# Reciprocal root by a power on GpSimd, and columns spread by transposition, in a two-block mixer network

## The chip, the cores and the metric

The kernel runs on one core of a Trainium2 chip. The core has five engines with queues of their own: TensorE (PE in the profile; its weight loads are PEld), VectorE (DVE), ScalarE (ACT), GpSimd (POOL) and SyncE (SP), which issues most DMAs. The metric is the device time of one execution in microseconds; lower is better.

## What is computed

The input is x of 512 tokens with 1024 features and a context of 256 tokens. A first block mixes tokens by retention and by an mLSTM, both in two directions, and ends in a gated feed-forward part; a second block has four layers: latent attention, windowed attention, long convolutions, latent attention. What matters here are the norms, which stand at many places (before and after each layer, per head behind the retention and the mLSTM, on the compressed queries and keys of the latent attention):

```python
def rms_norm(x, gain):
    xf = x.astype(jnp.float32)
    y = xf * lax.rsqrt(jnp.mean(xf * xf, axis=-1, keepdims=True) + EPS)
    return (y * gain.astype(jnp.float32)).astype(x.dtype)

def head_norm(t):
    tf = t.astype(jnp.float32)
    return tf * lax.rsqrt(jnp.mean(tf * tf, axis=-1, keepdims=True) + EPS)
```

Also of matter are the places where a number per token divides a whole row: the sums of the softmax in both attentions, and the denominator of the mLSTM, h = num / max(|den|, exp(-m)).

## The kernel before

Activations lie with the features on the partitions and the tokens along the free axis, in tiles of [128, 512] for x and [128, 256] for the context. Every fp32 operand of the large products is kept as two halves (a rounded one and the rest), so a product is three matmuls (`mac`, L438 to L440). Weights come by DMA from SyncE's queue and are split into halves by ScalarE (L394) and VectorE (L395).

A norm goes in three steps. `Rms.add` squares a tile on ScalarE (L231) and sums on VectorE (L235). `Rms.root` turns the sums into a column per 128 tokens: on TensorE the sum over the partitions, with the tile of sums as stationary operand and a column of ones as moving one (L242); on ScalarE the root with its scale and eps (L244); on VectorE the reciprocal (L245). `Rms.rstd` then calls `over_columns`, which spreads columns over the partitions: column j, repeated 128 times by its access pattern, is the stationary operand, the identity is the moving one, and the fp32 product has the column along the free axis of every partition (L1370). VectorE multiplies with it (L567 in `apply`, L1305 behind a mixer's output product, L899 for the heads).

There are 44 roots, 13 of four columns and 31 of two, so 114 columns named rs. `over_columns` has three other callers: the latent attention (L1602) spreads the reciprocal sums of the softmax (rd) with four columns per head for x and, in the first of its layers, two per head for the context; the windowed attention (L1741) spreads four per unit, of which there are 24 (6 for each of 4 groups); the mLSTM (L1015) spreads its denominators (den), four columns for each of 4 heads and 2 directions. That makes 176 columns of rd and 32 of den.

The order of work is written with generators: `weave` lets several streams take turns at given shares, so that the steps of a norm stand between the products of another stream. Constants such as D5, D6, E0 and E2 set how many steps lie between a root and its use. At the end of a layer (`layer_end`), the product of one group of 256 tokens is woven with the norm of the group before. The framework that builds the program then sets the order on each engine's queue from the order of the code and an estimate of its own, and puts in the waits and ScalarE's table loads.

Of the kernel before, what the change touches and what calls it, by code (L numbers as in the profile page):

```python
# [18 lines left out]
D = 1024  # L19
# [158 lines left out]
def mix(*items):  # L178
    """Takes turns between generators: (generator, its number of steps), each at its share."""
    live = [[g, n, 0] for g, n in items if g is not None and n]  # L180
    while live:
        x = min(live, key=lambda x: x[2] / x[1])
        try:
            next(x[0])
        except StopIteration:
            live.remove(x)
            continue
        x[2] += 1
        yield
# [7 lines left out]
def idle(n):  # L197
    """Steps without work."""
    for _ in range(n):
        yield  # L200
# [21 lines left out]
class Rms:  # L222
    """Sums of squares over the partitions of some tiles [128, n]."""

    def __init__(self, k, n, width, eps=None):
        self.k, self.n, self.width, self.acc, self.cols = k, n, width, None, None
        self.eps = k.eps if eps is None else eps
# [9 lines left out]
    def root(self):  # L237
        """Columns of 1/rms: tokens on the partitions."""
        nc, nt = self.k.nc, self.n // 128
        ps = self.k.mm()  # L240
        for j in range(nt):
            nc.tensor.matmul(ps[:, j:j + 1], self.acc[:, 128 * j:128 * j + 128], self.k.ones1, start=True, stop=True)  # L242
        s = self.k.sp.tile([128, 8], F32, tag="rs", name="rs")
        nc.scalar.activation(s[:, :nt], ps[:, :nt], AF.Sqrt, bias=self.eps, scale=1.0 / self.width)  # L244
        nc.vector.reciprocal(s[:, 4:4 + nt], s[:, :nt])  # L245
        self.cols = [s[:, 4 + j:5 + j] for j in range(nt)]

    def rstd(self):
        """PSUM [128, n] of 1/rms on every partition."""
        if self.cols is None:  # L250
            self.root()
        return self.k.over_columns(self.cols, 128)


class Kern:
# [15 lines left out]
    def setup(self):  # L271
# [28 lines left out]
        self.eps = self.cp.tile([128, 1], F32, name="eps")  # L300
        nc.vector.memset(self.eps, EPS)
        self.eps4 = self.cp.tile([128, 1], F32, name="eps4")
        nc.vector.memset(self.eps4, 4 * EPS)
# [15 lines left out]
    def rows(self, late, dma):  # L319
        """Columns of the small vectors, of the first group or the others."""  # L320
# [23 lines left out]
        if not late:  # L344
            # silu of the conditioning vectors as padded stationary columns
# [34 lines left out]
    def acts(self, kt, n):  # L380
        """kt feature tiles [128, n] in two halves."""
# [15 lines left out]
    def wload(self, W, r0, kt, c0, n):  # L397
        """Rows r0.. (kt tiles) and columns c0.. of W, f32 [128, kt, n]."""
# [9 lines left out]
    def wm(self, W, r0, kt, c0, n=128):  # L408
        """kt tiles [128, n] of W in two exact halves."""
# [4 lines left out]
    def wheld(self, W, c0, slot, r0=0, kt=KT):  # L414
        """wm of 128 columns, held in two to four tiles of another pool if one is given."""
# [13 lines left out]
    def wv(self, W, c0):  # L429
        """The same for 256 columns of all D rows."""  # L430
        return self.wm(W, 0, 4, c0, 256) + self.wm(W, 512, 4, c0, 256)

    def mac(self, ps, pairs, start=True, stop=True):
        """ps (+)= sum over pairs (l, r) of l^T r with both halves of each."""
# [7 lines left out]
    def proj(self, w, act, n, c0=0, m=128):  # L442
        """PSUM [m, n] = (columns c0.. of w)^T act, act [kt] of [128, n]."""
# [4 lines left out]
    def proj_t(self, act, t0, w, ps):  # L448
        """ps [128 tokens, cols] = act[:, t0..]^T w."""
        self.mac(ps, [(a[:, t0:t0 + 128], x) for x, a in zip(w, act)])  # L450

    def lead(self, loads, h, late, first=None):
        """PSUM [128, N] of three products (of weights, 128 columns) with h; `late` makes its second half of tokens, `first` runs before."""
# [19 lines left out]
    def load_T(self, src, n, dst):  # L473
        """Feature tiles dst[k] [128, n] of src [n, D]."""
# [17 lines left out]
    def mod(self, W, w0, cond, bias, dst_x, dst_c):  # L492
        """Columns w0..w0+1023 of W (f32, [1024, .]) applied to both conditioning vectors, plus bias columns."""
# [23 lines left out]
    def mod_stream(self):  # L517
        """All modulation vectors in their order of use, in steps."""
# [21 lines left out]
    def mods(self, n):  # L540
        """The next n steps of the stream, as an item to weave."""
# [7 lines left out]
    def rstd(self, xs, n, width):  # L549
        """PSUM [128, n] of 1/rms over the partitions and tiles of xs."""  # L550
# [5 lines left out]
    def rstd1(self, x, f):  # L556
        """Head norm sums of one tile, to be finished later: 1 / sqrt(f * mean + 4 * eps)."""
        r = Rms(self, N, DH / f, self.eps4)
# [3 lines left out]
    def apply(self, x, bc, n, G, S, dst, kt):  # L562
        """dst halves = x * G * bc + S, per feature tile; S None: no shift."""
# [35 lines left out]
    # ================= first block =================  # L599
    def first_block(self):  # L600
# [68 lines left out]
        def gates():  # L669
# [27 lines left out]
            # rows, forward on [0:4] and backward on [32:36]: input gates, log forget gates  # L697
            # (context: halves of one tile)
# [37 lines left out]
            # rows to spread over the partitions: B - m on [0:64], exp(B + m0 - m) on [64:128]  # L736
# [5 lines left out]
            # columns: exp(-m)  # L742
# [7 lines left out]
            # columns: exp(i - B + ...) of the context, i - B of x  # L750
# [32 lines left out]
        def kv_ctx(w):  # L783
            """Token-major keys or values of the context for a pair of heads, f32 [128, 2, 256]."""
# [10 lines left out]
        def dense(pair, ml):  # L795
            """Projections of two heads: K, V, the context's states, q, gate."""
# [80 lines left out]
        def scores(K, q):  # L877
            """S^T of all blocks: four PSUM banks [128 keys, N]."""
# [16 lines left out]
        def finish():  # L895
            """The head norm of the head before."""
# [4 lines left out]
        def ret_chain(pair):  # L901
            o = out[pair, False]
            for u in range(2):
                h = 2 * pair + u
                # decays between tokens on two overlapping strips, columns 0..511 and 384..895
# [46 lines left out]
        def ml_chain(pair):  # L952
            o = out[pair, True]
            for u in range(2):
# [46 lines left out]
                for d in range(2):  # L1001
                    # 1 / max(|den|, exp(-m)) with the tokens on the partitions: the rows of den are all the same
# [80 lines left out]
        def passes(W, r0, kt, act, gate, slots, rs, ws):  # L1083
            """X += gate * act^T W for the first half of the tokens, then for the other."""
# [83 lines left out]
        def norm3(g):  # L1168
            """The first block's last norm, and the next layer's."""
# [22 lines left out]
    # ================= second block =================  # L1192
# [20 lines left out]
    def keep(self, i, k, x, t0):  # L1213
        """Halves of the tokens t0.. of tile k (6 or 7) of a mixer's output, for its product."""
# [8 lines left out]
    def preload(self, l, W):  # L1223
        """The first weights of a mixer's output product."""
# [7 lines left out]
    def load_acts(self, i, t0, a):  # L1232
        """Halves of 256 tokens of the mixer's output tiles that are in DRAM, two tiles in one."""
# [7 lines left out]
    def layer_end(self, l, W, tail):  # L1241
        """Output product of a layer's mixer, the residuals, and the norm of the next layer, in groups of 256 tokens: the last one's pending.
        The mixer's last steps are woven with the first product."""
# [86 lines left out]
    def store(self, ys, t0, c0):  # L1330
        """256 tokens of four feature tiles to the output."""
# [16 lines left out]
    def rope64(self, ps):  # L1348
        """ps [128 = two heads of 64, N] with the axial rotation, f32."""
# [8 lines left out]
    def stacks(self, r, n, d0, d1):  # L1358
        """Halves of two heads of 64 rows over each other: d0 = [hi; lo] of r[0:64], d1 = [lo; hi] of r[64:128]."""
# [6 lines left out]
    def over_columns(self, cols, m):  # L1366
        """PSUM [m, 128 * len]: each column [128, 1] along the free axis of every partition."""
        ps = self.mm()
        for i, c in enumerate(cols):
            self.nc.tensor.matmul(ps[:m, 128 * i:128 * i + 128], c.to_broadcast([128, m]), self.ident, start=True, stop=True)  # L1370
        return ps[:m, :128 * len(cols)]

    def softmax(self, S, P, rd, scale, sink=None):
        """P = exp(scale * S - its maximum), rd = 1 / its sums over the free axis (with a further column `sink`)."""
# [13 lines left out]
    def transposed(self, blocks):  # L1388
        """[128, 128 * len] halves of the transposes of f32 blocks [128, 128]."""
# [8 lines left out]
    def stream_tiles(self, items, lag):  # L1398
        """Dense tiles: items of (weights, use for x, use for the context or None), the context's `lag` tiles behind;
# [703 lines left out]
```

## Time and profile before

| what | us |
|---|---|
| median of 3 runs | 2951.34 (2949.51 to 2959.04) |
| span of the profiled execution | 2954.9 |
| TensorE busy in it | 2825.0 (96%) |
| VectorE busy | 1819.6 (62%) |
| ScalarE busy | 1395.2 (47%) |
| GpSimd busy | 85.8 (3%) |

The rows further down come from one profiled execution. In its views, a row of a timeline gives the start of a group of instructions, their length, engine, line, operation, what is written and read, the count, and in brackets how long the engine had been idle and what ended that. Matmuls overlap, so what one costs is read from the distance between starts, not from its length. An engine's busy share is an average over stretches with different limits, so the table of stretches is read beside it.

### The profile page before, as it was taken

Reading aid. Unit: us, or ns where it says so; the run is one execution under the profiler, and the core shown is the slowest. Engines: PE = TensorE matmul, PEld = TensorE weight load, DVE = VectorE, ACT = ScalarE, POOL = GpSimd, SP = SyncE. Lnnn points to the kernel's source line nnn. Section 1 sums busy time; section 2 is a strip of 40 time slices with the busy share of each in tenths; the row PEclk is TensorE's granted clock in tenths of the full one; section 3 lists DMA queues with packets and bytes.
Section 4 is the critical chain, followed back from the end, with each engine's and each line's share of the span. In section 5 each row is a group of like instructions: output and inputs, shape, how many; then the busy total and the mean of one; then the engine's idle time right before and its main releaser. Section 6 shows DMA issues by size and latency. Waiting matters only on the chain. (4 is left out here: it accounts for less than half of the span.)

```text
span 2954.9 us, 44726 instructions
## 1 busy us (share of the span) xinstructions
PE 2825.0 (96%) x17428; PEld 2408.8 (82%) x17428; DVE 1819.6 (62%) x3772; ACT 1395.2 (47%) x2692; POOL 85.8 (3%) x113
## 2 busy tenths in 40 slices
PE   6999999999999999999999998998999998999998
PEld 4888888887777787888889877778988886987887
DVE  6655455555655556246667577787676676844774
ACT  5344445346455343445555566665332222644553
POOL 0000000000000000000000000000012121000000
PEclk9999999999999999999999999999999999999998
DMA  7333232544555537211234141123223225431122
GB/s 260 87 119 111 78 93 80 167 152 140 166 157 168 165 100 234 87 58 49 72 99 140 60 129 43 33 64 96 85 81 97 76 81 188 147 91 61 58 76 68
DMA packets 365831, 319.01 MB, mean 108 GB/s; under 512 B 17511, under 2 KB 326517, under 8 KB 365620
## 3 DMA queue, kind: packets, MB, share of 16 engines
q1 hardware_dynamic: 365204, 315.99, 34.5%
q8 instruction: 137, 2.24, 0.3%
q0 software_dynamic: 416, 0.17, 0.1%
q14 instruction: 74, 0.61, 0.1%
HBM read 273.90 MB, written 42.21 MB: 107 GB/s over the span
## 5 line engine op out<-in xcount | busy, mean ns | idle before, releaser
L438 PE MATMUL mm<-b,whi 128*128 128x512 f32 (+1 forms) x2548 | 896.1, 352 | 3.3 <-ACT whi L394 1.6
L439 PE MATMUL mm<-b,whi 128*128 128x512 f32 (+1 forms) x2548 | 888.2, 349 | 0.5 <-DVE b L573 0.5
L440 PE MATMUL mm<-b,wlo 128*128 128x512 f32 (+1 forms) x2548 | 887.4, 348 | 1.2 <-DVE wlo L395 1.2
L438 PEld LDWEIGHTS mm<-b,whi 128*128 128x128 f32 x2548 | 486.3, 191 | 72.5 <-issue 5.0
L440 PEld LDWEIGHTS mm<-b,wlo 128*128 128x128 f32 x2548 | 486.2, 191 | 62.0 <-DVE wlo L395 2.1
L439 PEld LDWEIGHTS mm<-b,whi 128*128 128x128 f32 x2548 | 486.7, 191 | 61.1 <-issue 1.2
L395 DVE TENSOR_TENSOR wlo<-raw,whi 128x1024 fp32r<-128x1024 f32 (+3 forms) x286 | 292.2, 1023 | 265.2 <-ACT whi L394 251.8
L394 ACT CAST whi<-raw 128x1024 fp32r<-128x1024 f32 (+3 forms) x286 | 252.5, 885 | 366.7 <-PE mm L439 239.7
L440 PE MATMUL mm<-b 128*128 128x256 f32 (+1 forms) x628 | 190.7, 304 | 0.5 <-DVE b L395 0.3
L1382 ACT ACTIVATE P<-mm,sm 128x768 f32<-128x768 f32 (+3 forms) x176 | 128.0, 728 | 121.4 <-DVE sm L1379 75.2
L438 PE MATMUL mm<-b 128*128 128x256 f32 (+1 forms) x500 | 159.3, 320 | 8.1 <-ACT P L1382 4.3
L438 PE MATMUL mm<-b,P 128*128 128x256 f32 x560 | 161.6, 288 | 4.2 <-ACT b L572 3.6
L439 PE MATMUL mm<-b,P 128*128 128x256 f32 x560 | 159.3, 284 | 0.3 <-DVE b L573 0.3
L1377 DVE TENSOR_REDUCE sm<-mm 128x1 f32<-128x768 f32 (+3 forms) x176 | 128.6, 733 | 46.4 <-PE mm L1580 25.6
L439 PE MATMUL mm<-b 128*128 128x256 f32 (+1 forms) x500 | 154.2, 309 | 0.4 <-DVE b L395 0.3
L395 DVE TENSOR_TENSOR t<-mm,t 128x512 fp32r<-128x512 f32 (+1 forms) x208 | 136.8, 664 | 15.0 <-ACT t L394 13.6
L235 DVE TENSOR_TENSOR t<-t 128x256 f32<-128x256 f32 (+1 forms) x216 | 93.0, 441 | 81.9 <-ACT t L231 79.0
L394 ACT CAST t<-mm 128x512 fp32r<-128x512 f32 (+1 forms) x208 | 116.0, 570 | 54.6 <-PE mm L1392 51.2
L231 ACT ACTIVATE t<-b 128x256 f32<-128x256 f32 (+1 forms) x252 | 101.3, 431 | 70.7 <-DVE b L1098 38.1
L1392 PE MATMUL mm<-ct,P 128*128 128x128 f32 x768 | 121.6, 276 | 11.7 <-ACT P L1382 7.3
L440 PEld LDWEIGHTS mm<-b 128*128 128x128 f32 x628 | 121.4, 193 | 5.7 <-DVE b L395 1.3
L440 PE MATMUL mm<-b,P 128*128 128x256 f32 x432 | 122.9, 284 | 0.0
(358 smaller groups left out, 5159.5 us busy)
## 6 DMA issues: line engine op xcount, KB each, us to landing
raw<-in_w_mod_dram SPq DMA_DIRECT2D x96, 512.0 KB, 4.7
raw<-in_w_ada_dram SPq DMA_DIRECT2D x48, 512.0 KB, 3.7
raw<-in_w_in_dram SPq DMA_DIRECT2D x48, 512.0 KB, 3.8
raw<-in_w_ffn_in_dram SPq DMA_DIRECT2D x44, 512.0 KB, 3.8
raw<-in_c_w_in_dram SPq DMA_DIRECT2D x32, 512.0 KB, 4.2
raw<-in_a_w_in_dram SPq DMA_DIRECT2D x28, 512.0 KB, 4.1
ks<-t SPq DMA_DIRECT2D x48, 256.0 KB, 2.8
raw<-ks SPq DMA_DIRECT2D x24, 512.0 KB, 3.6
```

Source lines behind the costliest of these rows:

```text
L231: self.k.nc.scalar.activation(sq, x, AF.Square)
L235: self.k.nc.vector.tensor_tensor(self.acc, self.acc, sq, ALU.add)
L394: self.nc.scalar.copy(dst.hi, src)
L395: self.nc.vector.tensor_tensor(dst.lo, src, dst.hi.bitcast(F32), ALU.subtract)
L438: nc.tensor.matmul(ps, l.hi, r.hi, start=start and i == 0, stop=False)
L439: nc.tensor.matmul(ps, l.hi, r.lo, start=False, stop=False)
L440: nc.tensor.matmul(ps, l.lo, r.hi, start=False, stop=stop and i == n - 1)
L1377: nc.vector.tensor_reduce(s[:, 0:1], S, AX.X, ALU.max)
L1382: nc.scalar.activation(P, S, AF.Exp, bias=s[:, 1:2], scale=scale, accum_out=s[:, 2:3])
L1392: self.nc.tensor.transpose(ps[:, 128 * i:128 * i + 128], b, self.ident)
```

## The change

Three things change. The scale 1/width of the mean goes into the column of ones, of which there is now one for each width. Eps is added on VectorE, straight from PSUM, and the power -0.5 is taken on GpSimd with a constant tile of exponents; the root on ScalarE and the reciprocal on VectorE are gone. And `over_columns` uses the transposition of TensorE with the repeated column as the tile that is transposed, in place of the fp32 product. Comments and doc strings go too; no constant of the weaving changes. Later lines move down by 3.

```diff
 class Rms:
-    def __init__(self, k, n, width, eps=None):
+    def __init__(self, k, n, width, eps=EPS):
...
-        self.eps = k.eps if eps is None else eps
+        self.eps = eps
...
     def root(self):
...
-            nc.tensor.matmul(ps[:, j:j + 1], self.acc[:, 128 * j:128 * j + 128], self.k.ones1, start=True, stop=True)
+            nc.tensor.matmul(ps[:, j:j + 1], self.acc[:, 128 * j:128 * j + 128], self.k.means[self.width], start=True, stop=True)
         s = self.k.sp.tile([128, 8], F32, tag="rs", name="rs")
-        nc.scalar.activation(s[:, :nt], ps[:, :nt], AF.Sqrt, bias=self.eps, scale=1.0 / self.width)
-        nc.vector.reciprocal(s[:, 4:4 + nt], s[:, :nt])
+        nc.vector.tensor_scalar(s[:, :nt], ps[:, :nt], self.eps, None, ALU.add)
+        nc.gpsimd.tensor_tensor(s[:, 4:4 + nt], s[:, :nt], self.k.mhalf[:, :nt], ALU.pow)
...
-        self.eps = self.cp.tile([128, 1], F32, name="eps")
-        nc.vector.memset(self.eps, EPS)
-        self.eps4 = self.cp.tile([128, 1], F32, name="eps4")
-        nc.vector.memset(self.eps4, 4 * EPS)
+        self.means = {}
+        for width in (D, 512, 256, DH, DH // 4):
+            self.means[width] = self.cp.tile([128, 1], F32, name=f"mean{width}")
+            nc.vector.memset(self.means[width], 1.0 / width)
+        self.mhalf = self.cp.tile([128, 4], F32, name="mhalf")
+        nc.gpsimd.memset(self.mhalf, -0.5)
...
-        r = Rms(self, N, DH / f, self.eps4)
+        r = Rms(self, N, DH // f, 4 * EPS)
...
     def over_columns(self, cols, m):
...
-            self.nc.tensor.matmul(ps[:m, 128 * i:128 * i + 128], c.to_broadcast([128, m]), self.ident, start=True, stop=True)
+            self.nc.tensor.transpose(ps[:m, 128 * i:128 * i + 128], c.to_broadcast([128, m]), self.ident)
```

The order on the engines is set anew. On ScalarE, at the end of the windowed attention's layer (L1274 copies the product of the mixer's output from PSUM, L231 squares it), the queue read before:

```order
1559 L394 CAST b<-t 128x128 x2
1560 L1274 COPY b<-mm 128x256
1561 L244 ACT_TABLE_LOAD
1562 L244 ACTIVATE rs<-mm,eps 128x2
1563 L231 ACTIVATE t<-b 128x256 x3
```

and now:

```order
1494 L1744 ACTIVATE t<-mm 128x512
1495 L1277 COPY b<-mm 128x256
1496 L397 CAST b<-t 128x128 x2
1497 L231 ACTIVATE t<-b 128x256
1498 L1277 COPY b<-mm 128x256
```

The table load and the root are gone; over the whole queue there were 75 table loads and are 37.

On VectorE at the same place (rs is the column of the root, L1749 and L395 are the last steps of the windowed attention, L1305 uses the spread column), the queue read before:

```order
2263 L1746 TENSOR_TENSOR t<-t 64x256 x2
2264 L1749 TENSOR_TENSOR t<-t,b 128x128 x2
2265 L395 TENSOR_TENSOR b<-t,b 128x128 x2
2266 L245 RECIPROCAL rs<-rs 128x2
2267 L1305 SCALAR_TENSOR_TENSOR b<-b,mod_7293,mm 128x256 x4
```

and now:

```order
2265 L1749 TENSOR_TENSOR t<-t 64x256 x2
2266 L1752 TENSOR_TENSOR t<-t,b 128x128 x2
2267 L244 TENSOR_SCALAR rs<-mm 128x2
2268 L398 TENSOR_TENSOR b<-t,b 128x128 x2
2269 L1308 SCALAR_TENSOR_TENSOR b<-b,mod_7301,mm 128x256 x5
```

The addition of eps stands two rows ahead of the place that the reciprocal had. At other roots it has moved by none to four rows. On GpSimd the first powers stand behind the DMA issues of the start and ahead of the long convolutions' sums:

```order
17 L339 DMA rows<-in_c_conv_b_dram 12x128 x2
18 L339 DMA rows<-in_c_filt_bias_dram 16x128
19 L245 ISA
20 L245 TENSOR_TENSOR rs<-rs,mhalf 128x4
21 L245 TENSOR_TENSOR rs<-rs,mhalf 128x2
22 L245 TENSOR_TENSOR rs<-rs,mhalf 128x4 x8
23 L245 TENSOR_TENSOR rs<-rs,mhalf 128x2 x8
24 L245 TENSOR_TENSOR rs<-rs,mhalf 128x4 x2
25 L245 TENSOR_TENSOR rs<-rs,mhalf 128x2 x13
26 L1995 TENSOR_TENSOR t<-t 128x256
```

All 44 powers are there, 33 of them ahead of the first sum of the long convolutions (L1995); before, the queue went from the DMA issues to those sums.

## Rows read from the trace of the kernel before

**Rows 1.** The page: busy us and share by engine, and granted clock in tenths.
```profile
PE 2825.0 (96%) x17428; PEld 2408.8 (82%) x17428; DVE 1819.6 (62%) x3772; ACT 1395.2 (47%) x2692; POOL 85.8 (3%) x113
...
PEclk9999999999999999999999999999999999999998
```

**Rows 2.** Busy us by stretch: mLSTM, latent attention, windowed attention; then clock, DMA.
```profile
core 0: us, PE busy (x) PEld busy (x) DVE busy (x) ACT busy (x) POOL busy (x), PEclk, DMA share, GB/s
340.00:500.00 160.00, 156.49 (x865) 128.92 (x864) 84.59 (x166) 74.15 (x138) 0.00 (x0) 0.97 0.30 87
1360.00:1500.00 140.00, 138.96 (x870) 120.86 (x870) 96.80 (x215) 75.51 (x162) 0.00 (x0) 1.00 0.23 70
1690.00:2018.00 328.00, 300.04 (x1937) 254.96 (x1937) 248.37 (x673) 205.56 (x506) 0.00 (x0) 0.98 0.22 64
```

**Rows 3.** TensorE's waits over the span: us in total, times, longest.
```profile
PE mm L1370 <- DVE rs L245: 18.8, 11, 2.4
```

**Rows 4.** Instructions of L1370 (the column spread): duration ns min/median/max, first and last start.
```profile
L1370 PE MATMUL mm<-ct,rd x352: 270/275/421, 1350.4 to 2886.0; 128*128 128x128 f32 x176
...
L1370 PE MATMUL mm<-ct,rs x228: 270/275/583, 52.7 to 2942.2; 128*128 128x128 f32 x114
...
L1370 PE MATMUL mm<-ct,den x64: 270/275/376, 342.5 to 498.9; 128*128 128x128 f32 x64
```

**Rows 5.** Timeline of TensorE around a spread and around four transposes: start, us.
```profile
1429.35 1.05 PE L1370 MATMUL mm<-ct,rd 128*128 128x128 f32 x8
...
1430.36 0.28 PE L439 MATMUL mm<-b 128*128 128x256 f32 x1
1430.47 0.29 PE L440 MATMUL mm<-b 128*128 128x256 f32 x1
...
1423.16 0.60 PE L1392 MATMUL mm<-ct,P 128*128 128x128 f32 x4
...
1423.83 0.40 PE L439 MATMUL mm<-t,b 128*128 128x512 f32 x1
1424.07 0.39 PE L440 MATMUL mm<-t,b 128*128 128x512 f32 x1
```

**Rows 6.** TensorE's waits in the windowed attention, 1690 to 2018.
```profile
PE mm L1710 <- ACT P L1382: 10.0, 12, 1.6
PE mm L1738 <- DVE t L395: 7.5, 9, 2.1
```

**Rows 7.** Root and reciprocal over the span: duration ns min/median/max.
```profile
L244 ACT ACTIVATE rs<-mm,eps x44: 262/263/268, 44.5 to 2941.3; 128x2 f32<-128x2 f32 x31, 128x4 f32<-128x4 f32 x13
L244 ACT ACT_TABLE_LOAD  x21: 1283/1283/1283, 42.9 to 2913.0; - x21
...
L245 DVE RECIPROCAL rs<-rs x44: 154/166/179, 45.4 to 2941.6; 128x2 f32<-128x2 f32 x31, 128x4 f32<-128x4 f32 x13
```

**Rows 8.** Timeline of a root at the end of the windowed attention's layer.
```profile
2021.56 0.50 PE L242 MATMUL mm<-ones,t 128*128 128x1 f32 x4
...
2022.55 1.28 ACT L244 ACT_TABLE_LOAD   x1
2023.84 0.26 ACT L244 ACTIVATE rs<-mm,eps 128x2 f32<-128x2 f32 x1
...
2024.14 0.17 DVE L245 RECIPROCAL rs<-rs 128x2 f32<-128x2 f32 x1 [1.55 <-ACT rs L244]
...
2024.36 0.71 PE L1370 MATMUL mm<-ct,rs 128*128 128x128 f32 x4 [2.29 <-DVE rs L245]
```

**Rows 9.** GpSimd: its smallest group (busy us, mean ns), and L1992's durations.
```profile
L2089 POOL MEMSET const-float32-1.0<- 128x1 f32 x1 | 0.1, 99 | 0.0
...
L1992 POOL TENSOR_TENSOR P<-t x16: 723/743/1727, 2172.7 to 2483.5; 128x256 f32<-128x256 f32 x16
```

**Rows 10.** Stretches behind waits of L1370: busy us, clock; one of four, and the sum.
```profile
2025.28:2028.69 3.41, 3.41 (x19) 3.41 (x18) 3.41 (x10) 0.75 (x2) 0.00 (x0) 0.50 0.10 36
...
sum 17.05, PE 16.09 PEld 16.10 DVE 13.35 ACT 1.72 POOL 0.00; mean PE 4.02 PEld 4.02 DVE 3.34 ACT 0.43 POOL 0.00
```

**Rows 11.** Transposes of L1392 alone in the latent attention: busy us, clock.
```profile
1360.00:1500.00 140.00, 24.11 (x154) 18.33 (x155) 1.00 0.23 70
```

## The prediction

> **What bounds the kernel now.** I read the page's busy shares and its row of granted clocks first, then the busy time by stretch, then TensorE's waits, then the rows of the lines that the change touches. TensorE is busy in 96% of the span at nearly the full clock; VectorE stands at 62%, ScalarE at 47% [rows 1]. By stretch [rows 2] the share is 156.5 of 160 us in the mLSTM part and 139 of 140 in the latent attention, but 300 of 328 in the windowed attention, where VectorE is at 76%. So an instruction less on TensorE is worth its whole price nearly everywhere, and less in the windowed attention. The largest single wait of TensorE is the one that the change goes at: the column spread of L1370 waits 18.8 us, in 11 places, for the reciprocal of L245 [rows 3].
>
> **Part 1: columns by transposition.** The spread (L1370) issues one fp32 product of 128 columns per column of numbers. The trace has 228, 352 and 64 matmul records for rs, rd and den [rows 4]; the program has half as many, so each product runs as two. Transposes of L1392 have the same operands (ct moving, a 128x128 fp32 tile stationary), and there a call for four blocks leaves four records. Price of each [rows 5]: four spread columns begin at 1429.35, the second instruction behind them at 1430.36, that is 1.01 us, of which 0.12 belong to the 256-column matmul between: 0.89. Four transposes begin at 1423.16, the second instruction behind at 1423.83, 0.67 us less 0.23 for a 512-column matmul: 0.44. So four columns save 0.45 us. There are 114 + 176 + 32 = 322 columns, 80.5 fours: 36 us of TensorE at most.
>
> Of these, 96 columns (24 units of four) lie in the windowed attention: 10.8 us. There TensorE waits most for the softmax (10.0 us, 12 times) and for splits on VectorE (7.5 us, 9 times) [rows 6]; a saving just ahead of such a wait is eaten by it. I take half, 5.4. The other 226 columns (25.4 us) stand mostly where TensorE is 98 to 99% busy; I take 95%, 24.1, the rest for the start and one den group that a wait follows. **Part 1: -29.5 us**, with -20 (windowed attention nothing, elsewhere 80%) and -36 as its ends.
>
> **Part 2: the root.** The chain now is ones products (L242), root on ScalarE, reciprocal on VectorE, spread. On ScalarE the root takes 0.26 us, and 21 of 44 need a table load of 1.28 us first; the reciprocal takes 0.17 [rows 7]. At 2021.6 one sees it whole [rows 8]: products over at 2022.06, a copy and the table load until 2023.84, root, reciprocal until 2024.31, spread at 2024.36 after 2.29 us of idle TensorE.
>
> After the change VectorE adds eps (one for one with the reciprocal, 0.17 us), GpSimd takes the power, TensorE goes on. Three hand-overs of about 0.05 us each, as between L245 and L1370 in [rows 8], make 0.32 us plus the power. No row shows a power on GpSimd. Its bounds are GpSimd's MEMSET of one element, 0.10 us, and the longest two-input TENSOR_TENSOR of 256 elements, 1.73 us; the median of the latter is 0.74 [rows 9]. The new one has two inputs and only 2 or 4 elements, but a power is many steps per element; I take 0.6, near that median and a little under it. In a sentence that the rest can do without: the Trainium skill (GPSIMD Engine Reference, 3.1 Elementwise) has an addition of two tensors 1.96 times as long on GpSimd as on VectorE and calls GpSimd the wrong place for elementwise work; twice the reciprocal would make 0.33 us here and the whole sum 4.6 us better, but no run here shows a power.
>
> Who feels it is read from the order of TensorE's instructions. In nine roots the spread stands right behind the ones products, in two there are two products of 0.12 us between, in six there are four or five in the new order; the other 27 have 17 or more products (2 us and up) as cover. With p for the power, the nine wait p + 0.32 each, the two p + 0.09, the six about p - 0.25. That is 17 p + 1.6 us. At p = 0.6 it is 11.8 against 18.8 now: **part 2: -7 us**; at 0.10, where the six wait no more, about -14; at 1.73 +12; it breaks even at p = 1.0. VectorE's queue helps: the add no longer waits for ScalarE, so it is set up to four rows ahead of where the reciprocal stood, past two splits at 2022 and past four rows of the long convolution's end. The rows that it passes then wait for the ones products; at 2022 that is 0.1 us, covered by VectorE's idle time of 1.55 us there [rows 8]. If the addition takes 0.1 us more because it reads PSUM, that is 1.7 us.
>
> **Part 3: the clock.** Right behind four of these eleven waits the granted clock stood at 0.50, the 1.2 GHz level, for 17.05 us in sum [rows 10], which costs half of that, 8.5 us. Waits of about 0.9 us in their place should lose some of these stretches: I take **-3 us**, between 0 and -8.5.
>
> **At nothing.** ScalarE loses 44 roots and 38 table loads (75 before, 37 after, by its order), some 60 us; it is at 47%, the softmax waits hold no table load, and the wait that it ended is counted in part 2. The new constants are five small MEMSETs for two on VectorE and one on GpSimd, under the first loads. GpSimd's queue has only its DMA issues (over at 8.6 us) ahead of the first power, and no power is issued while the long convolutions use it. The ones products keep their shape.
>
> **Sum.** -29.5 - 7 - 3 = -39.5 us: the profiled span of 2954.9 would be 2915.4. The span lies 3.6 us (0.12%) above the median of the runs, 2951.34; I take the difference over to the median: **2912 us**.
>
> **Rivals.** *The power takes 1.0 to 2.7 us.* For it: nothing in the trace shows its price, and the longest small row of GpSimd is 1.73. Against it: only 2 to 4 elements. At 1.73 us part 2 is +12 instead of -7 and the clock gives nothing back: -29.5 + 12 = -17.5, 2934 us; the case spans 2922 to 2951.
>
> *The power is so slow that the kernel loses.* The place is the nine layer-end roots with the spread right behind the sums. The waits reach 18.8 + 29.5 = 48 us, all that part 1 gives, at p = 2.7. At 4 us the 17 roots wait 17 x 4 + 1.6 = 70, and twelve roots whose cover is 24 products of 0.12 us (2.8 us) wait 1.5 us each: 88 in all, +69 - 29.5 = +40, 2991 us. It decides from 2.7 us, over three times the median of 256-element additions.
>
> *The columns don't give their time.* Either the broadcast column makes the transpose run as two passes like the product (then part 1 is zero: -10, 2941), or waits in the attentions eat most of it (part 1 at -18: -28, 2923). Against the first: the product has the same broadcast operand, and the transposes beside it run in one. Against the second: TensorE at 99% in the latent attention [rows 2].
>
> *Transposes pull the clock down.* In the stretch 1360 to 1500, 24.1 us of TensorE's work are transposes, and the granted clock is 1.00 throughout [rows 11]. A shortest half-clock stretch is 3.41 us and costs 1.7; there are 100 spreads, and if every tenth drew one it would cost 17 us: -39.5 + 17 = -22, 2929 us; if every fourth, the gain is gone. A rule stands behind this one: the Trainium skill (TensorE: Matmul & The Clock Gate, Part 4: PE-mode transpose) says that transposes do not count as TensorE being busy in the same way, so that the full clock does not engage for them; the row above speaks against it where they are mixed with matmuls.
>
> **How the numbers follow.** Forecast 56%, spread over 2893 to 2922 by the ends of the three parts (all at their best, -36 - 14 - 8.5 = -58.5, to part 1 at its worst); the power at 1.0 to 2.7 us 18%; slower 10%; columns that don't pay 12%; clock 4%. From 2898 to 2944 lie 53 of the first, 13 of the second, 11 of the fourth and 3 of the fifth: 80. About 0.3% (8.9 us) is what a measurement can tell from no change: faster is below 2942.5. To it go 56, 13 of the second, 9 of the fourth, 2 of the last: 0.80. Within 0.3%: 4 + 3 + 1, about 0.09; slower: the 10 and 1: 0.11.
>
> **What would show it.** In the profile of the changed kernel the spread's matmul records should be 322 instead of 644, and four of them with the next start some 0.45 us shorter. The power's row on GpSimd gives p at once; TensorE's wait for it should be near 12 us in sum, with 0.9 us at the layer ends. ScalarE's table loads should be 37. In the windowed attention the length from the same first to the same last matmul should shrink by about 5 us, and the half-clock stretches behind the layer ends should be fewer. A power above 1 us, a windowed attention as long as before, or new half-clock stretches would make the prediction wrong, and so would reordered products elsewhere, since the order of each engine is set anew at the build.

## The result and the profile after

The changed kernel takes 2917.95 us (median; 2914.05 to 2920.95), the kernel before 2952.49 us in the same series (2949.51 to 2959.04). The ratio is 0.9885, with a 95% interval of 0.9872 to 0.9898: 34 us less, or 1.1%. The forecast was 2912 us with a range of 2898 to 2944. In the profiled execution the span is 2917.0 us after 2954.9, so 37.9 us less, 3.4 more than the medians give: the profiled execution of the kernel before was a long one.

The page of the changed kernel, busy us and share by engine, answers to [rows 1]:

```profile
PE 2787.1 (96%) x17106; PEld 2364.2 (81%) x17106; DVE 1814.9 (62%) x3775; ACT 1334.4 (46%) x2610; POOL 128.8 (4%) x158
```

TensorE is busy for 37.9 us less, which is the whole difference of the spans. The rest of the span, in which TensorE does nothing, is 129.9 us in both traces. So the time left TensorE's own work and, in sum, none of it TensorE's waiting.

The spread's instructions in the changed kernel, duration in ns (min/median/max), first and last start, as in [rows 4]; and in the second fence a spread on TensorE's timeline, as in [rows 5]:

```profile
L1373 PE MATMUL mm<-ct,rd x176: 270/272/421, 1339.9 to 2850.4; 128*128 128x128 f32 x176
L1373 PE MATMUL mm<-ct,rs x114: 270/272/476, 52.8 to 2904.3; 128*128 128x128 f32 x114
L1373 PE MATMUL mm<-ct,den x32: 270/272/322, 340.9 to 491.9; 128*128 128x128 f32 x32
```

```profile
1417.21 0.60 PE L1373 MATMUL mm<-ct,rd 128*128 128x128 f32 x4
1417.56 0.36 PE L441 MATMUL mm<-b 128*128 128x256 f32 x1
1417.76 0.28 PE L442 MATMUL mm<-b 128*128 128x256 f32 x1
```

There are 322 records for 644. From the start of four spread columns to the second instruction behind them it is 0.55 us; less 0.12 for the 256-column matmul between, 0.43 is left, where the fp32 products took 0.89.

The root's two new instructions over the span (the answer to [rows 7]); then, in a fence of their own, TensorE's waits over the span (us in total, times, longest; compare [rows 3] and [rows 6]):

```profile
L244 DVE TENSOR_SCALAR rs<-mm x44: 142/159/164, 44.6 to 2903.1; 128x2 f32<-128x2 f32 x31, 128x4 f32<-128x4 f32 x13
...
L245 POOL TENSOR_TENSOR rs<-rs,mhalf x44: 695/844/1955, 44.9 to 2903.4; 128x2 f32<-128x2 f32 x31, 128x4 f32<-128x4 f32 x13
```

```profile
PE mm L1373 <- POOL rs L245: 15.8, 17, 1.5
PE mm L1713 <- ACT P L1385: 9.5, 11, 1.6
...
PE mm L1741 <- DVE t L398: 7.9, 10, 2.0
...
PE mm L242 <- DVE t L235: 4.4, 4, 2.3
```

In the kernel before, the two rows that answer to the last two of these were:

```profile
PE mm L1738 <- DVE t L395: 8.3, 10, 2.1
...
PE mm L242 <- DVE t L235: 2.7, 4, 1.4
```

The power takes 0.70 us for two columns where VectorE leaves it alone, 1.01 for four, and up to 1.96 (the last section shows what VectorE has to do with it). TensorE waits for it in 17 places, 15.8 us in sum, where it waited 18.8 in 11. The same root as in [rows 8], on the timeline of the changed kernel (start, us, in brackets the idle time and what ended it):

```profile
1992.82 0.50 PE L242 MATMUL mm<-mean,t 128*128 128x1 f32 x4
...
1993.43 0.16 DVE L244 TENSOR_SCALAR rs<-mm 128x2 f32<-128x2 f32 x1
...
1993.67 0.80 POOL L245 TENSOR_TENSOR rs<-rs,mhalf 128x2 f32<-128x2 f32 x1 [386.20 <-DVE rs L244]
...
1994.52 0.43 PE L1373 MATMUL mm<-ct,rs 128*128 128x128 f32 x2 [1.20 <-POOL rs L245]
```

There the chain is 1.20 us for 2.29. Elsewhere it appeared where there had been none. In the windowed attention, from its first score product to its last output product, busy us by engine, granted clock and DMA share, first of the kernel before and then of the changed one:

```profile
1670.70:2017.70 347.00, 317.40 (x2050) 268.01 (x2048) 260.86 (x711) 216.10 (x536) 0.00 (x0) 0.98 0.23 68
```

```profile
1652.20:1989.20 337.00, 306.61 (x1955) 256.06 (x1953) 260.04 (x711) 216.15 (x535) 0.00 (x0) 0.97 0.24 70
```

TensorE's work fell by 10.8 us and the stretch by 10.0: next to nothing was eaten there.

### The profile page after: what moved, and what is told of

Read it like the earlier page. It is cut to its first block, busy times and chain, and to the rows that moved or that the text cites. A ratio compares the mean times of both kernels' runs of the same rounds, so it can differ in the third digit from the quotient of the medians.

```text
span 2917.0 us, 44103 instructions
## 1 busy us (share of the span) xinstructions
PE 2787.1 (96%) x17106; PEld 2364.2 (81%) x17106; DVE 1814.9 (62%) x3775; ACT 1334.4 (46%) x2610; POOL 128.8 (4%) x158
## 5 line engine op out<-in xcount | busy, mean ns | idle before, releaser
L398 DVE TENSOR_TENSOR wlo<-raw,whi 128x1024 fp32r<-128x1024 f32 (+3 forms) x286 | 292.0, 1023 | 239.7 <-ACT whi L397 224.1
L1385 ACT ACTIVATE P<-mm,sm 128x768 f32<-128x768 f32 (+3 forms) x176 | 127.9, 727 | 116.6 <-DVE sm L1382 68.4
L441 PE MATMUL mm<-b,P 128*128 128x256 f32 x560 | 161.8, 289 | 4.0 <-ACT b L575 2.8
L442 PE MATMUL mm<-b,P 128*128 128x256 f32 x560 | 160.4, 286 | 0.9 <-DVE b L576 0.8
L1380 DVE TENSOR_REDUCE sm<-mm 128x1 f32<-128x768 f32 (+3 forms) x176 | 128.6, 733 | 39.7 <-PE mm L1583 23.8
L245 POOL TENSOR_TENSOR rs<-rs,mhalf 128x2 f32<-128x2 f32 (+1 forms) x44 | 42.3, 962 | 2427.2 <-DVE rs L244 2279.8
L398 DVE TENSOR_TENSOR t<-mm,t 128x512 fp32r<-128x512 f32 (+1 forms) x208 | 136.5, 663 | 15.3 <-ACT t L397 14.1
L235 DVE TENSOR_TENSOR t<-t 128x256 f32<-128x256 f32 (+1 forms) x216 | 92.5, 441 | 71.9 <-ACT t L231 69.4
L231 ACT ACTIVATE t<-b 128x256 f32<-128x256 f32 (+1 forms) x252 | 100.7, 431 | 67.7 <-DVE b L1101 40.9
```

What stands on the lines that cost most here:

```text
L231: self.k.nc.scalar.activation(sq, x, AF.Square)
L235: self.k.nc.vector.tensor_tensor(self.acc, self.acc, sq, ALU.add)
L245: nc.gpsimd.tensor_tensor(s[:, 4:4 + nt], s[:, :nt], self.k.mhalf[:, :nt], ALU.pow)
L398: self.nc.vector.tensor_tensor(dst.lo, src, dst.hi.bitcast(F32), ALU.subtract)
L441: nc.tensor.matmul(ps, l.hi, r.hi, start=start and i == 0, stop=False)
L442: nc.tensor.matmul(ps, l.hi, r.lo, start=False, stop=False)
```

## Experiments

Each ran in a series with the kernel before, and its ratio is to the kernel before of that series. The last column is (ratio - 1) x 2951 us, so it can be compared between series; an interval of 0.0015 on either side is 4.4 us, and a difference of two rows is uncertain by some 5 us.

| kernel | median us | ratio (95%) | against before, us |
|---|---|---|---|
| changed | 2917.95 | 0.9885 (0.9872 to 0.9898) | -33.9 |
| changed, again | 2918.45 | 0.9886 (0.9870 to 0.9902) | -33.6 |
| columns alone | 2914.65 | 0.9876 (0.9862 to 0.9891) | -36.6 |
| root alone | 2953.26 | 1.0004 (0.9995 to 1.0013) | +1.2 |
| changed, products in the window | 2926.09 | 0.9919 (0.9906 to 0.9931) | -23.9 |
| changed, root ahead of the addition | 2938.44 | 0.9957 (0.9942 to 0.9973) | -12.7 |
| changed, root beside the power | 2921.36 | 0.9887 (0.9872 to 0.9903) | -33.3 |
| changed, two powers | 2937.67 | 0.9936 (0.9923 to 0.9949) | -18.9 |
| changed, product for power | 2904.90 | 0.9847 (0.9831 to 0.9863) | -45.2 |
| changed, D2 = 1 | 2920.00 | 0.9886 (0.9871 to 0.9901) | -33.6 |
| columns, D2 = 1 | 2922.70 | 0.9892 (0.9879 to 0.9906) | -31.9 |
| changed, D2 = 4 | 2932.34 | 0.9939 (0.9925 to 0.9953) | -18.0 |
| columns, D2 = 4 | 2926.95 | 0.9925 (0.9909 to 0.9941) | -22.1 |

**Columns alone**, on the kernel before:

```diff
-            self.nc.tensor.matmul(ps[:m, 128 * i:128 * i + 128], c.to_broadcast([128, m]), self.ident, start=True, stop=True)
+            self.nc.tensor.transpose(ps[:m, 128 * i:128 * i + 128], c.to_broadcast([128, m]), self.ident)
```

> The kernel before with the transpositions alone; root and reciprocal stay on ScalarE and VectorE. My theory: the columns carry nearly all of the gain, and the windowed attention gives up its whole 10.8 us instead of the half that I took (its length fell by 10.0 us in the changed kernel). Then the span falls by about 33 us (28 to 36), the windowed attention by about 10, and TensorE still waits near 18.8 us for the reciprocal. Rival: the columns give only some 15 us here, because waits for the root eat the rest, and the gain of 38 us needs both parts together.

It gained 36.6 us (32 to 41), as much as the whole change and a little more than I expected. TensorE's wait for the reciprocal stayed (us in total, times, longest):

```profile
PE mm L1370 <- DVE rs L245: 19.2, 12, 2.6
```

The windowed attention took 335.7 us, 11.3 less:

```profile
1655.00:1990.70 335.70, 305.26 (x1956) 254.84 (x1954) 259.79 (x711) 216.35 (x535) 0.00 (x0) 0.98 0.24 71
```

The rival falls: the columns need no help from the root.

**Root alone**: the diff above the other way round, on the changed kernel.

> The changed kernel with the columns spread by fp32 products again; the power on GpSimd stays. My theory: the power takes 0.96 us in the mean, not 0.6, so it lies close to its break-even of 1.0, and TensorE's waits for the root only go from 18.8 to about 16 us: 3 to 6 us less than before in all. Rival A: the 60 us that ScalarE is rid of are worth something elsewhere (splits and copies that come earlier), 12 us or more, up to 20. Rival B: slower than before by 3 us or more, since 17 roots now have a wait in place of 11.

No gain: +1.2 us, with an interval of -1.5 to +3.8. The 3 to 6 us less that I expected lie outside, and so does rival A; of rival B (slower by 3 us or more) only the edge lies inside. TensorE's waits, where the second row was 2.7 us in 4 places before:

```profile
PE mm L1373 <- POOL rs L245: 16.4, 18, 1.5
...
PE mm L242 <- DVE t L235: 3.1, 4, 1.4
```

The waits for the root fell by 2.4 us, as expected; that much did not show in the time. What cancelled it is below what these runs can tell.

**Products in the windowed attention alone**: `over_columns` of the changed kernel gets a flag, set at L1744, for the fp32 product.

> The changed kernel with fp32 products for the 96 columns of the windowed attention alone. My theory: that part has no slack for a shorter TensorE, so it gets back its whole price, +10 us against the changed kernel (9 to 11), all of it between the first and the last matmul of the windowed attention. Rival, the prediction's step: half is eaten by waits for softmax and splits, +5 us. A second rival: the 10 us came from ScalarE's relief in that part and not from the columns, then +5 or less as well, but with e1 showing less than 6 us there.

It gave back 10.0 us, nearly the price of its 24 units, 24 x 0.45 = 10.8. The windowed attention, in the view used above:

```profile
1650.90:1998.10 347.20, 317.18 (x2050) 267.86 (x2048) 260.92 (x711) 216.20 (x536) 0.00 (x0) 0.98 0.23 68
```

347.2 us, to a fifth of a microsecond the length before the change. Both rivals fall: no half is eaten, and ScalarE's relief has no part in it, since the columns alone, without that relief, shortened the stretch by 11.3.

**A root ahead of the addition**:

```diff
-        s = self.k.sp.tile([128, 8], F32, tag="rs", name="rs")
+        s = self.k.sp.tile([128, 8], F32, tag="rs", name="rs"); u = self.k.sp.tile([128, 4], F32, tag="us", name="us"); nc.scalar.activation(u[:, :nt], ps[:, :nt], AF.Sqrt)
```

> The changed kernel with a root on ScalarE beside each power, whose result nothing reads, so that ScalarE gets its 44 roots and its table loads back. My theory: ScalarE has room, the prediction's 'at nothing' holds: 0 to +3 us against the changed kernel. Rival: ScalarE's 60 us were part of the gain, by splits and copies that stood behind table loads: +10 us or more.

21 us slower than the changed kernel, which looks like the rival. The timeline of the same root as above shows that the experiment had another effect than the one I meant:

```profile
2008.60 0.50 PE L242 MATMUL mm<-mean,t 128*128 128x1 f32 x4
...
2009.90 1.28 ACT L243 ACT_TABLE_LOAD   x1
...
2011.20 0.17 ACT L243 ACTIVATE us<-mm 128x2 f32<-128x2 f32 x1
...
2011.47 0.16 DVE L244 TENSOR_SCALAR rs<-mm 128x2 f32<-128x2 f32 x1 [1.57 <-ACT us L243]
2011.71 0.70 POOL L245 TENSOR_TENSOR rs<-rs,mhalf 128x2 f32<-128x2 f32 x1 [386.51 <-DVE rs L244]
2012.46 0.47 PE L1373 MATMUL mm<-ct,rs 128*128 128x128 f32 x1 [3.35 <-POOL rs L245]
```

The addition reads the same PSUM tile as the root and started behind it: VectorE's idle 1.57 us ended with the root. So the chain held both. The waits for the power rose to 28.7 us in 16 places, 12.9 more, and the half-clock time rose from 109.9 us (96.9 in a second profile of the changed kernel, further down) to 131.3. So this run doesn't say what ScalarE's work costs by itself; the next one does.

**A root beside the power**: the same, behind the addition and from its result in SBUF.

> The changed kernel with a root on ScalarE that reads the column behind the addition, in SBUF, and whose result nothing reads: ScalarE gets its 44 roots and 75 table loads back, and nothing stands in front of the addition or the power (in the earlier run the root read the same PSUM tile as the addition, and the addition started 1 to 2.7 us later, behind it). My theory: TensorE's waits for the power stay near 16 us, the time stays within 4 us of the changed kernel (2914 to 2922). Rival: ScalarE's 60 us are worth something by themselves: +8 us or more with the waits for the power unchanged.

The time is that of the changed kernel (+0.6 us), with ScalarE back at its work. The page's busy us, and then TensorE's wait for the power:

```profile
PE 2791.3 (95%) x17106; PEld 2369.4 (81%) x17106; DVE 1817.1 (62%) x3775; ACT 1391.6 (48%) x2692; POOL 129.0 (4%) x158
```

```profile
PE mm L1373 <- POOL rs L245: 17.9, 17, 2.2
```

57 us of ScalarE's work, table loads among it, cost nothing off the chain that these runs can tell; the waits are 2 us above what I expected.

**Two powers**:

```diff
-        nc.gpsimd.tensor_tensor(s[:, 4:4 + nt], s[:, :nt], self.k.mhalf[:, :nt], ALU.pow)
+        nc.gpsimd.tensor_tensor(s[:, :nt], s[:, :nt], self.k.mhalf[:, :nt], ALU.pow); nc.gpsimd.tensor_tensor(s[:, 4:4 + nt], s[:, :nt], self.k.mone[:, :nt], ALU.pow)
```

> The changed kernel with a second power on GpSimd behind each first one (exponent 1, so nothing changes in value). It measures what a slower GpSimd step costs, which is the slope of my part 2: 17 roots with no cover of their own times 0.7 to 0.9 us gives 12 to 15 us of wait more (15.8 to about 29), the other 27 have 1.7 us or more of cover and give little: +12 to +18 us against the changed kernel, 2930 to 2936. Rival: the waits are mostly taken from other waits behind them (splits, softmax) and the slope is small: +5 us or less.

15.0 us slower, in the middle of the expectation. The two powers' durations (as for L245 above), and TensorE's wait:

```profile
L245 POOL TENSOR_TENSOR rs<-rs,mhalf x44: 695/857/1957, 44.6 to 2916.0; 128x2 f32<-128x2 f32 x31, 128x4 f32<-128x4 f32 x13
L245 POOL TENSOR_TENSOR rs<-rs,mone x44: 695/707/1659, 45.7 to 2916.7; 128x2 f32<-128x2 f32 x31, 128x4 f32<-128x4 f32 x13
```

```profile
PE mm L1373 <- POOL rs L245: 29.2, 18, 2.5
```

The waits rose by 13.4 us, so a microsecond of this wait costs about one of time (15.0 / 13.4 = 1.1, with some 5 us of uncertainty on the 15.0).

**The changed kernel again**, and beside it **a product for the power**: `ALU.mult` for `ALU.pow`, and `mhalf` is zero, so all norms come out as zero.

> The changed kernel once more, unchanged, as the one that the other three are compared with. Expected: 0.9885 of the kernel before, as measured (0.987 to 0.990), and TensorE's waits for the power at 15.8 us within 1 us.

> The changed kernel with a product by a column of zeros on GpSimd in place of the power: same operands, same shape, so all norms come out as zero and only the time means something. It tells what of the 0.70 us (2 columns) and 1.01 us (4 columns) is the power and what any small operation on GpSimd costs. Theory A: the power itself is dear; a product of 2 columns takes 0.1 to 0.25 us, the waits fall from 15.8 to about 17 x 0.15 + 1.6 = 4 to 6 us, and the time falls by about 10 us. Theory B: the fixed cost of an operation on GpSimd is most of it, 0.5 us or more, and the time stays within 4 us.

The repetition gave 0.9886 and 15.8 us of waits. The product gave 11.5 us less than that. Its durations, and TensorE's wait for it:

```profile
L245 POOL TENSOR_TENSOR rs<-rs,mhalf x44: 194/198/1147, 46.8 to 2895.2; 128x2 f32<-128x2 f32 x31, 128x4 f32<-128x4 f32 x13
```

```profile
PE mm L1373 <- POOL rs L245: 7.4, 11, 1.0
```

Theory A holds, though the waits fell less far than to the 4 to 6 us that I expected. A product of two or four columns costs 0.20 us on GpSimd; the power makes 0.70 and 1.01 of it. The slope is there in this direction as well: 8.4 us of wait less, 11.5 us of time, which agrees with one for one within the intervals.

**One step more between root and spread** at the layer ends, on the changed kernel and on the columns alone:

```diff
-D2 = 0
+D2 = 1
```

> The changed kernel with D2 at 1 for 0: one step of products stands between root and spread at the layer ends. My theory: the seven waits there (0.76, 1.10, 1.20, 1.10, 1.42, 1.53, 1.10 us, 8.2 in all) go to zero and TensorE's time falls by as much, 6 to 8 us against the changed kernel (about 2911). Rival: the step only moves the wait, because the norm that follows comes later by as much and the next layer's first product waits for it: 0 to 2 us, or slower.

> The kernel before with the transpositions and D2 at 1 for 0; root and reciprocal stay on ScalarE and VectorE. My theory: it gains more from the step than the changed kernel does, since its layer-end waits are the longer ones (about 2 us each where a table load lies in the chain, 1.6 in the mean): 6 to 12 us less than the transpositions alone (2914.65), 2903 to 2909. Rival: one step of products (about 1.4 us) does not cover the root with its table load, and the norm that comes later gives it back: 0 to 4 us.

Nothing gained by the first (+0.3 us), and nothing by the second either: it stands 4.7 us behind the columns alone, with intervals that overlap, and the 6 to 12 us less that I expected are excluded. In the first the seven waits that I had named stayed (1.10, 1.20, 1.41 and so on), because the spread was still taken in the same turn of the weaving as the root. What did move was another kind of root, in front of the next layer: three waits of 0.34 to 0.52 us went. The waits of the changed kernel with D2 = 1, then of the columns with D2 = 1:

```profile
PE mm L1373 <- POOL rs L245: 14.2, 14, 1.5
...
PE mm L242 <- DVE t L235: 9.1, 8, 2.9
```

```profile
PE mm L1370 <- DVE rs L245: 19.0, 11, 2.6
...
PE mm L242 <- DVE t L235: 7.5, 5, 2.5
```

TensorE now waits longer for the sums of the next norm (L242 for L235): 9.1 us after 4.4, and 7.5 after 2.5 in the columns alone.

**Four steps more**: D2 = 4, on the same two kernels, where the order has 21 or more products between sums and spread at seven layer ends.

> The changed kernel with D2 at 4 for 0. With 1 the order at the layer ends did not change (root and spread are taken in the same turn), which is why the earlier run left those waits at 0.76 to 1.53 us. With 4 the order has 21 to 24 products between sums and spread at seven layer-end roots and 24 or more at three others, but none any more at three that had 24. So 8.2 + 1.4 us of waits go and about 3.3 come: theory A, 5 to 8 us less than the changed kernel (0.983 of before). Theory B: the step moves the wait to the sums of the next norm (TensorE for L235 on VectorE), as it did with D2 at 1 (4.4 to 9.1 us there): 0 to 2 us, or slower.

> The kernel before with the transpositions and D2 at 4; root and reciprocal stay on ScalarE and VectorE. Its order has 24 products (2.8 us) between sums and spread where the changed kernel has them. Theory A: ScalarE's root with its table load (about 2 us) is covered there, 6 to 10 us less than the transpositions alone (0.9876), so 0.984 or less, and then the power on GpSimd is needed for nothing. Theory B: the norm that comes later gives it back, and the time stays at 0.987 to 0.989.

Both became slower: by 15.6 us against the changed kernel of the same series, by 14.5 against the columns alone. The waits of the first and of the second:

```profile
PE mm L242 <- DVE t L235: 18.6, 11, 3.8
...
PE mm L1373 <- POOL rs L245: 9.4, 10, 1.5
```

```profile
PE mm L242 <- DVE t L235: 19.2, 11, 4.0
...
PE mm L1370 <- DVE rs L245: 6.3, 6, 2.4
```

The waits for the root did shrink, by 6.4 and 12.9 us, and those for the next norm's sums grew by 14.3 and 16.7. That is theory B's mechanism in both, at a higher price than it named for the second (0.9925 for 0.987 to 0.989). The clock has a part in it. In the changed kernel TensorE does nothing for 140.6 us of the span with D2 = 4 and for 129.7 in the repetition with D2 = 0, 10.9 more; and it is busy for 2792.8 us after 2781.1, 11.7 more for the same 17106 instructions, with 124.8 us at half clock after 96.9. Together that is the 22.6 us by which the two spans differ (2933.4 and 2910.8). These are single profiles, but the granted clock of the whole span is lower in every execution: 0.978 to 0.981 in five with D2 = 4, 0.982 to 0.984 in four of the repetition.

No version that still computes the norms beats the changed kernel beyond the intervals; the columns alone, with root and reciprocal left where they were, are as fast.

## Why the prediction was right, and which steps were not

**What bounds the kernel: right.** TensorE's 37.9 us of work are the 37.9 us of the span, and the columns alone, which take work from TensorE and nothing else, give all of it. The largest single wait of the profile, 18.8 us, looked like the aim of the change and gave next to nothing of the time.

**Part 1, columns: right in kind, too small in size.** The price held (0.43 against my 0.44 for four transpositions; 322 records). The term was -29.5 us and measured -36.6, which is 80.5 fours at their full 0.45 us. The step that failed is the half that I struck off in the windowed attention, because TensorE waits there for the softmax and for splits [rows 6]. Those waits stayed almost whole (10.0 to 9.5 and 8.3 to 7.9 over the stretch), and the stretch is 10.0 us shorter; putting the products back there restored the length. That they eat next to nothing is shown; why is read from the waits, and no run isolates it: the softmax itself waits for TensorE. What ScalarE and VectorE wait for in that stretch of the changed kernel (us in total, times, longest):

```profile
ACT P L1385 <- DVE sm L1384: 39.3, 35, 3.2
...
DVE sm L1380 <- PE mm L1719: 7.8, 10, 2.2
DVE sm L1380 <- PE mm L1713: 6.9, 5, 2.3
```

The exponential (L1385) waits for VectorE's scaled maxima (L1384) in 35 places, and the maxima (L1380) wait for the score products on TensorE in 15. On this reading a shorter TensorE brings forward what it will wait for, and a wait would swallow the saving only if what ends it ran independently of TensorE; VectorE, busy for 260 of 337 us, was not what set the pace.

**Part 2, the root: the formula held, the power was mis-sized, and the gain is not to be seen.** I took 0.6 us, near the median of GpSimd's 256-element additions [rows 9]. In the 17 places where TensorE waits it takes 0.80 us in the mean (0.96 over all 44). The count of 17 was right, and 17 x 0.80 + 1.6 = 15.2 us against 15.8 measured. So the term should have been -3 for -7. The row that I took as nearest was far in both respects, more elements and a cheaper operation: a product of these small shapes takes 0.20 us, the power three and a half to five times that. That 0.6 came as near as it did to 0.70 was luck, since the two errors went opposite ways. Of the -3 us not even that shows in time: alone the root gave +1.2 us (-1.5 to +3.8), and the columns with it are at 0.9885 against 0.9876 without. TensorE's wait for the next sums, L242 for L235, rose from 2.7 to 4.4 us in the changed kernel, which offsets about half of it there, but only from 2.7 to 3.1 with the root alone. What cancels the rest stays open; it is within the intervals. Two powers and the product for the power agree with the slope in both directions. My break-even of 1.0 us was on the waits alone; in time it lies about where the power is.

A sentence that the rest can do without: the Trainium skill (GPSIMD Engine Reference, 3.1 Elementwise) has an addition of two tensors of 2048 elements 1.96 times as long on GpSimd as on VectorE; here the small product stands at 0.198 us against 0.159 for VectorE's addition of eps, 1.2 times, and the power of two columns at 4.4 times, so the ratio of the page fits neither.

**Part 3, the clock: not shown.** In the first profile the four stretches of [rows 10] are gone, 17.05 us, but others came: the half-clock time of the whole span went from 112.5 to 109.9 us only, which is 1.3 us of time and not 3. The busy us of all half-clock stretches, as in [rows 10]: the sum for the changed kernel in its first profile, then in the repetition of the same program:

```profile
sum 109.90, PE 92.63 PEld 68.57 DVE 63.00 ACT 32.66 POOL 6.58; mean PE 4.63 PEld 3.43 DVE 3.15 ACT 1.63 POOL 0.33
```

```profile
sum 96.90, PE 80.10 PEld 59.72 DVE 56.05 ACT 25.78 POOL 6.09; mean PE 4.22 PEld 3.14 DVE 2.95 ACT 1.36 POOL 0.32
```

Between two executions of one program it differs by 13.0 us, and half of that is 6.5, about the 6.2 us by which their spans differ (2917.0 and 2910.8). A term of 3 us for the clock can't be read from one profile on either side. Nor is it settled that the stretches behind these waits are gone: behind waits for the power stand 3.4 us of half clock in the first profile (at 1102.43, behind the wait that ends at 1101.86) and 10.2 in the second, after 17.05.

**At nothing: right.** ScalarE lost 60.8 us and 38 of 75 table loads, and it could have kept them: with its roots back beside the power the time did not change by more than the intervals allow. It mattered only as a link of the chain, as the run with the root ahead of the addition shows.

**The rivals.** The power between 1.0 and 2.7 us: not where TensorE waits, by the mean (0.80, with three of the 17 at 1.08 to 1.20), though four columns take 1.01 and some powers twice that, under cover. The power above 2.7: no. Columns that don't pay: no, they paid in full. Transpositions that pull the clock down: the clock of the span is 0.982 after 0.981. Beside it, the rule of the Trainium skill (TensorE: Matmul & The Clock Gate, Part 4: PE-mode transpose) would have cost time here, and with 322 transpositions mixed among products no loss appeared; what a long run of transpositions alone does is not shown.

So the mechanism and the size of the columns carried the forecast, but that the total of -39.5 us came out as near the measured -34 to -38 as it did was luck, since the parts missed in opposite directions: the columns by 7 us too little, root and clock by 10 or so too much.

## What to carry to other kernels

On an engine that is busy 96% of the time, price what the instructions on it cost and count them; before striking off a part because a wait stands behind it, see whether what ends that wait depends on this engine in turn, as it did here. An operation moved to an engine where it has not been seen needs a price from its own kind and its own size: here a power of two columns took 0.70 us, a product of two 0.20, an addition of 256 elements 0.74. And a wait that a norm causes can be pushed along by reordering: before moving a step, look at who waits for the work behind it.

## What was unexpected of the hardware

GpSimd's small operations stretch when they begin while VectorE works on two operands in SBUF. Three places on the changed kernel's timeline: one where VectorE is already splitting a weight (L398, both inputs in SBUF), one with VectorE reading PSUM (L996), with four columns in the power in both, and one, with two columns, where such a split begins after the power:

```profile
1186.74 1.22 DVE L398 TENSOR_TENSOR wlo<-raw,whi 128x1024 fp32r<-128x1024 f32 x1
1186.88 1.95 POOL L245 TENSOR_TENSOR rs<-rs,mhalf 128x4 f32<-128x4 f32 x1 [30.16 <-DVE rs L244]
...
364.87 1.01 POOL L245 TENSOR_TENSOR rs<-rs,mhalf 128x4 f32<-128x4 f32 x1 [52.57 <-DVE rs L244]
365.42 0.69 DVE L996 TENSOR_TENSOR t<-mm,t 128x512 f32<-128x512 f32 x1 [0.63 <-PE mm L443]
...
1057.59 0.70 POOL L245 TENSOR_TENSOR rs<-rs,mhalf 128x2 f32<-128x2 f32 x1 [425.44 <-DVE rs L244]
...
1057.72 0.96 DVE L398 TENSOR_TENSOR P<-raw,P 128x768 fp32r<-128x768 f32 x1 [0.21 <-ACT P L397]
```

The power takes 1.95 us beside the split, which runs for 1.09 us of it, and 1.01 beside the reader of PSUM. In the run with the product, the one at the same place takes 1.15 for 0.20, more by the same 0.95 us. At 1057.59 the split begins 0.13 us behind the power, and the power takes its 0.70. So what counts is the VectorE instruction that runs when GpSimd's begins. In all 18 places of this trace where that one has two inputs in SBUF, the power takes what is left of it and then 0.87 us for four columns or 0.55 to 0.57 for two (1.09 left makes 1.95, 0.57 left makes 1.12), as if it waited for its end; a VectorE instruction with an input in PSUM, or one that begins behind the power, adds nothing. TensorE feels it: its wait was 1.53 us at 1101.86, where such a split made the power of two columns take 1.12 us, and 1.10 where it took 0.70. The traces agree with what the Trainium skill says of this (GPSIMD Engine Reference, 1. Specifications): GpSimd shares its SBUF interfaces with VectorE and contends with VectorE instructions that have two SBUF inputs.

The other point is the order of readers: of two engines that read the same PSUM tile, one was placed behind the other in this program, and that put a table load of 1.28 us into a chain that needed none of it.
